# Attention scores as two full-height matmuls and two half-height ones, with the keys' halves placed to match and a new work plan

## The chip, the cores and the metric

The kernel runs on one core of a Trainium2 chip. The metric is the device time of one execution in microseconds. Before the change it was run three times, and one more execution was profiled.

## The reference, cut to what matters

One encoder layer works on two inputs, a prompt of 512 tokens and a sample of 1024 tokens, each token 1024 wide. RMSNorm is followed by one input projection whose columns are split into eight blocks. Group A is grouped-query attention (8 query heads, 2 key/value heads, 64 wide, normalised q and k, axial rotary). Group B is differential attention (4 heads with two softmax maps each, again 64 wide for q and k, 128 for v). Each group is gated by SiLU; the results are concatenated and projected back, the residual is added, and a last RMSNorm follows. The line that this change touches is the scores:

```
s = einsum('bqhgd,bkhd->bhgqk', q, k)          # group A, d = 64
s = einsum('bqhmd,bkhmd->bhmqk', q, k)         # group B, d = 64, two maps m
```

All values are float32.

## The kernel before, in words

Every float32 operand of a matmul is split into a high and a low half in float16, and products of halves are summed in float32. The projections use three products (high·high, high·low, low·high), one matmul each: `project_step`, lines 470 to 472.

For the scores, the contraction is only 64 long, so high and low are stacked: rows 0 to 63 of a q or k tile hold the high half of the 64 dimensions, and rows 64 to 127 hold the low half. `rows_high` (ACT) and `rows_low` (POOL) write these halves beside each other, a DMA transposes them, and q is stored to DRAM. `begin_tile` fetches q for one tile of 128 queries twice: `q1` as stored, and `q2` with the two halves of rows exchanged. One matmul of `q1` with the k tile sums high·high and low·low, one of `q2` sums low·high and high·low. A score op always fills two PSUM banks of 512 columns (`S[:, 0]` and `S[:, 1]`), so it is four matmuls of 128 rows, 128 columns of weights and 512 streamed columns, each with a weight load of its own: lines 1093, 1204 and 1205, 1241.

After a score op, DVE takes the row maximum (line 1098 or 1246), ACT takes the exponential (1109, 1255), in group B DVE combines two maps (1269), ACT and DVE or POOL split the result into halves (1064, 1067), a DMA transposes them into `pT` (1072), and PE multiplies `pT` with v: 24 small matmuls for one unit of work on the sample (lines 1122 to 1124 with 64 columns, 1283 to 1285 with 128).

The order of all work is computed when the kernel is built. Each piece is an `op` with an engine, an estimated duration, its inputs and its buffers; `Plan.schedule` plays the engines forward and writes the instructions out in that order. For PE the order comes from a list `seq`: attention units one after the other, the values of a unit `LAG` = 4 units behind its scores, and between them "fillers", the k steps (three matmuls each) of the projections ga, vb, kb, qb, gb and of the output projection. How many fillers come after each unit is set by `RATE_A` (group A, 80 units), `RATE_P` (group B, prompt, 16 units) and `RATE_S` (group B, sample, 32 units, two score ops each). The scores of group A make 80 score ops, those of group B 16 + 64, so 160 in all. There are 480 fillers for the projections and 200 for the output projection.

The stages on PE follow one another: the projections kva and qa; group A; group B on the prompt (called P below); group B on the sample (called S below); then the rest of the output projection.

Of the kernel before, what the change touches and what calls it, by code (L numbers as in the profile page):

```python
# [11 lines left out]
F16 = mybir.dt.float16  # L12
F32 = mybir.dt.float32
AF = mybir.ActivationFunctionType
ALU = mybir.AluOpType
AX = mybir.AxisListType

P = 128
D = 1024
KT = D // P  # L20
HD = 64
EPS = 1e-6
LAM_INIT = 0.8 - 0.6
NTP = 4
# [7 lines left out]
LAND = 1.0  # L32
SLACK = 1.03
NW = 15
RATE_A = 5.1
RATE_P = 4.0
RATE_S = 4.6
ET = mybir.EngineType
ALL = {ET.PE, ET.Activation, ET.DVE, ET.Pool, ET.SP}
MS = {ET.PE, ET.Activation, ET.DVE, ET.SP}  # L40
# [177 lines left out]
def kernel(ctx, tc, x_prompt, x_sample, g_norm, w_in, a_q_norm, a_k_norm,  # L218
                               lq1, lk1, lq2, lk2, b_subln, w_out, g_final, ropes, y_prompt, y_sample):
    nc = tc.nc  # L220
    ve, se, pe, ge, sy = nc.vector, nc.scalar, nc.tensor, nc.gpsimd, nc.sync
# [10 lines left out]
    qp = ctx.enter_context(tc.tile_pool(name="qp", bufs=2))  # L232
# [30 lines left out]
    k_a = [k_all[:, g] for g in range(3)]  # L263
# [222 lines left out]
    def pe_op(dur, fn, deps=(), uses=()):  # L486
        return op("PE", dur, fn, deps, uses)
# [285 lines left out]
    def rows_high(nh, box, kind="x4"):  # L773
        if kind == "x4":
            box["o2"] = rp.tile([P, 2, 8, P], F16, name="qk", tag="x4")
        elif kind == "xa":
            box["o2"] = tba.tile([P, 2, 8, P], F16, name="qka", bufs=2)
        else:
            box["o2"] = tba.tile([P, 1, 2, P], F16, name="kka", bufs=2)
        se.copy(box["o2"][:, 0, :nh, 0:HD], box["t1"][:, :nh, :])  # L780

    def rows_low(nh, box):
        o = box["o2"][:, 0]
        ge.tensor_tensor(out=o[:, :nh, HD:P], in0=box["t1"][:, :nh, :], in1=o[:, :nh, 0:HD], op=ALU.subtract)  # L784

    k_in, v_in, q_in = [None] * NT, [None] * NT, {}
    ka_b, va_b = buf("kav0"), buf("kav1")

    def post_kva(t, last, b):
        box = {}  # L790
        sq_b, t1_b, t2_b, x4_b = buf("sq"), buf("t1"), buf("t2"), buf("xk")
        tt, g, gi = t if t < NTP else t - NTP, t // 4, t % 4

        def vals():
            box["v"] = proj_ps["kva", t][:, P:2 * P].rearrange("p (h d) -> p h d", d=HD)
            box["k"] = proj_ps["kva", t][:, 0:P].rearrange("p (h d) -> p h d", d=HD)
            se.copy(v_a[t][:, :, 0:HD], box["v"])

        def vals_low():
            ve.tensor_tensor(out=v_a[t][:, :, HD:P], in0=box["v"], in1=v_a[t][:, :, 0:HD], op=ALU.subtract)  # L800

        def scale_rows():
            rope_add(2, box, ge)
            r = box["t1"]
            ge.tensor_tensor(out=r[:, :2, :], in0=r[:, :2, :],
                             in1=box["rs"].unsqueeze(2).broadcast_to([P, 2, HD]), op=ALU.mult)

        def turn():
            sy.dma_start_transpose(k_a[g][:, :, gi * P:(gi + 1) * P],
                                   box["o2"][:, 0, :2, :].rearrange("p h d -> p (h d)"))  # L810

        a = op("ACT", 0.25, vals, [last], [b])
        v_in[t] = op("DVE", 0.29, vals_low, [a], [b, va_b])
        s = op("ACT", 0.27, lambda: head_sums(box["k"], 2, box, "k"), [a], [b, sq_b])
        m = op("DVE", 0.55, lambda: head_var(2, box, "k", "eps_kva"), [s, w_ops["kva"][0]], [sq_b])
        r = op("POOL", 0.78, lambda: head_root(2, box, "k"), [m])
        ro = op("DVE", 0.6, lambda: rope_mult(box["k"], 2, rope_t["cak"][:, tt, :], rope_t["sak"][:, tt, :], 2, box),
                [a] + k_tables, [b, t1_b, t2_b])
        ad = op("POOL", 1.0, scale_rows, [ro, r], [t1_b, t2_b])
        h = op("ACT", 0.3, lambda: rows_high(2, box, "xk"), [ad], [t1_b, x4_b])  # L820
        lo = op("POOL", 0.43, lambda: rows_low(2, box), [h], [t1_b, x4_b])
        k_in[t] = op("SP", 0.4, turn, [lo], [x4_b, ka_b], kb=80, turn=True)
        tba_ops.extend((ro, k_in[t]))

    def post_rows(t, nm, last, b):

        box = {}
        nsub = 2 if nm == "qa" else 1
        kind = "xa" if nm == "qa" and t % 2 else "x4"
        t1_b, t2_b, x4_b = buf("t1"), buf("t2"), buf(kind)  # L830
# [202 lines left out]
    def begin_tile(t, half):  # L1033
        ts = TileState()
        ts.t, ts.half = t, half
        ts.T = 512 if t < NTP else 1024
        ts.kt0 = 0 if t < NTP else NTP
        ts.q_b, ts.o_b = buf("qp"), buf("O")
        ts.o = None

        def fetch():
            qd = q_dram[t][half]
            ts.q1 = qp.tile([P, 8, P], F16, name="q1")
            ts.q2 = qp.tile([P, 8, P], F16, name="q2")
            sy.dma_start(ts.q1, qd)
            sy.dma_start(ts.q2[0:HD], qd[HD:P])
            sy.dma_start(ts.q2[HD:P], qd[0:HD])
            ts.rs = tiny.tile([P, 8], F32, name="rs")

        ts.q_in = op("SP", 1.1, fetch, [q_in["qa" if half == 0 else "qb", t]], [ts.q_b], kb=512)  # L1050
        return ts

    def exps(st, i, p_i, S, w, ts, m, scale, nb):
        se.activation(p_i, S, AF.Exp, bias=nb, scale=scale, accum_out=ts.rs[:, m:m + 1])
# [26 lines left out]
    def plan_a(ts, hs):  # L1081
        t = ts.t
# [3 lines left out]

        def scores():
            st["S"] = ps_s.tile([P, 2, 512], F32, name="S", tag="S")
            for q, first in ((ts.q1, True), (ts.q2, False)):
                for j in range(2):  # L1090
                    h = hs[j % n]
                    g = 0 if t < NTP else 1 + j
                    pe.matmul(st["S"][:, j, :], q[:, h, :], k_a[g][:, h // 4, :], start=first, stop=not first)  # L1093

        def peak():
            S = st["S"]
# [27 lines left out]
                    pe.matmul(o, pT[:, 8 + c, :], v[:, kv, 0:HD], start=False, stop=(kt == nk - 1))  # L1124

        tiles = range(0, NTP) if t < NTP else range(NTP, NT)
        s = pe_op(0.87, scores, [ts.q_in] + [k_in[x] for x in tiles], [s_b, ts.q_b, ka_b])
        m = op("DVE", 1.4 if n == 1 else 1.55, peak, [s, qsc_in[t]], [s_b])
        e = op("ACT", 1.33 if n == 1 else 1.85, exp, [m], [s_b, p_b])
        tr, pT_b = plan_turn(st, e, p_b, "DVE")  # L1130
# [57 lines left out]
    def plan_b(ts, h):  # L1188
# [7 lines left out]
        if T == 512:  # L1196
# [2 lines left out]

            def scores():  # L1200
                st["S"] = ps_s.tile([P, 2, 512], F32, name="S", tag="S")
                for i in range(2):
                    kv = k_b[0, h][:, i, :]
                    pe.matmul(st["S"][:, i, :], ts.q1[:, 2 * h + i, :], kv, start=True, stop=False)
                    pe.matmul(st["S"][:, i, :], ts.q2[:, 2 * h + i, :], kv, start=False, stop=True)

            def peak():
                st["mx"] = tiny.tile([P, 2], F32, name="mx2")
# [10 lines left out]
                              accum_out=ts.rs[:, m:m + 1])  # L1219
                ps.append(p)  # L1220

            s = pe_op(0.87, scores, [ts.q_in] + ks, [s_b, ts.q_b] + kbufs)
            ss.append(s)
            m = op("DVE", 1.22, peak, [s, lam_in, w_ops["qb"][0]], [s_b])
            n = op("ACT", 0.38, bias, [m])
# [3 lines left out]
        else:  # L1229
            p_bs = []  # L1230
            for i in range(2):
# [4 lines left out]

                def scores(i=i, bx=bx):
                    bx["S"] = ps_s.tile([P, 2, 512], F32, name="S", tag="S")
                    for q, first in ((ts.q1, True), (ts.q2, False)):
                        for j, g in enumerate(groups):  # L1240
                            pe.matmul(bx["S"][:, j, :], q[:, 2 * h + i, :], k_b[g, h][:, i, :], start=first,  # L1241
                                      stop=not first)

                def peak(bx=bx):
                    bx["mx"] = tiny.tile([P, 1], F32, name="mx")
# [10 lines left out]
                                  accum_out=ts.rs[:, m:m + 1])  # L1256
                    ps.append(p)

                s = pe_op(0.87, scores, [ts.q_in] + ks, [s_b, ts.q_b] + kbufs)
                ss.append(s)  # L1260
                m = op("DVE", 1.22, peak, [s, lam_in, w_ops["qb"][0]], [s_b])
                n = op("ACT", 0.38, bias, [m])
# [232 lines left out]
    units = []  # L1495
    for t in range(NT):
        ts = begin_tile(t, 0)
        us = [plan_a(ts, hs) for hs in ([(h, h + 1) for h in range(0, 8, 2)] if t < NTP else [(h,) for h in range(8)])]
        plan_gate_a(ts, [u[2] for u in us], us[-1][1])
        units += [(u, RATE_A) for u in us]  # L1500
    for g in range(3):
# [71 lines left out]
```

## Time and profile before

| | before |
|---|---|
| median of 3 runs | 849.48 us (848.05 to 852.41) |
| profiled execution, its own time | 847.55 us |
| span from first to last instruction | 845.8 us |
| mean granted clock of TensorE | 0.987 |

The span is 1.75 us shorter than the profiled execution's time. In the profile, PE is TensorE's matmuls, PEld its weight loads, DVE, ACT and POOL the vector, scalar and GpSimd engines, SP the queue that issues every DMA. A matmul's row has a modelled end, so consecutive matmuls overlap in the rows, and their cost is read from start to start.

### The profile page before, as it was taken

Reading aid. Unit: us, or ns where it says so; the run is one execution under the profiler, and the core shown is the slowest. Engines: PE = TensorE matmul, PEld = TensorE weight load, DVE = VectorE, ACT = ScalarE, POOL = GpSimd, SP = SyncE. Lnnn points to the kernel's source line nnn. Section 1 sums busy time; section 2 is a strip of 40 time slices with the busy share of each in tenths; the row PEclk is TensorE's granted clock in tenths of the full one; section 3 lists DMA queues with packets and bytes.
Section 4 is the critical chain, followed back from the end, with each engine's and each line's share of the span. In section 5 each row is a group of like instructions: output and inputs, shape, how many; then the busy total and the mean of one; then the engine's idle time right before and its main releaser. Section 6 shows DMA issues by size and latency. Waiting matters only on the chain. (4 is left out here: it accounts for less than half of the span.)

```text
span 845.8 us, 16504 instructions
## 1 busy us (share of the span) xinstructions
PE 797.5 (94%) x6169; PEld 433.7 (51%) x6169; DVE 657.1 (78%) x1062; ACT 581.4 (69%) x1031; POOL 370.7 (44%) x377
## 2 busy tenths in 40 slices
PE   4999989999999999999999989899999999999885
PEld 2566634455555555555555445455555555555443
DVE  6888588687676878798777778677888999988832
ACT  6884259688568895567556866677888878777521
POOL 2689651000000104334253432345677777768830
PEclk9999989999999999999999999999999999999998
DMA  9999857999999999999999999989999988876942
GB/s 264 288 202 198 201 159 178 211 235 233 228 224 256 233 245 190 212 213 220 195 225 206 249 215 211 279 218 241 314 228 209 191 176 213 210 152 158 231 116 66
DMA packets 402448, 179.55 MB, mean 212 GB/s; under 512 B 364480, under 2 KB 365504, under 8 KB 402368
## 3 DMA queue, kind: packets, MB, share of 16 engines
q1 hardware_dynamic: 402368, 178.50, 94.5%
q8 instruction: 48, 0.79, 0.4%
q14 instruction: 32, 0.26, 0.1%
HBM read 62.33 MB, written 30.41 MB: 110 GB/s over the span
## 5 line engine op out<-in xcount | busy, mean ns | idle before, releaser
L1109 ACT ACTIVATE p<-S,nb,qsc 128x1024 f32<-128x1024 f32 (+1 forms) x96 | 101.4, 1058 | 74.1 <-DVE nb L1101 68.1
L1064 ACT CAST p<-p 128x1024 f16<-128x1024 f32 (+1 forms) x128 | 126.5, 989 | 35.5 <-DVE p L1269 22.2
L1098 DVE TENSOR_REDUCE mx<-S 128x1 f32<-128x1024 f32 (+1 forms) x80 | 97.5, 1219 | 31.9 <-PE S L1093 31.4
L1067 POOL TENSOR_TENSOR p<-p,p 128x1024 f16<-128x1024 f32 (+1 forms) x48 | 93.9, 1957 | 64.0 <-ACT p L1064 60.1
L1067 DVE TENSOR_TENSOR p<-p,p 128x1024 f16<-128x1024 f32 x80 | 102.4, 1282 | 23.5 <-ACT p L1064 23.1
L472 PEld LDWEIGHTS <-xT 128*128 128x128 f16 x672 | 66.2, 99 | 72.3 <-issue 3.1
L470 PEld LDWEIGHTS <-xT 128*128 128x128 f16 x672 | 66.7, 99 | 65.2 <-issue 5.6
L471 PEld LDWEIGHTS <-xT 128*128 128x128 f16 x672 | 66.2, 99 | 61.4 <-issue 3.7
L1246 DVE TENSOR_REDUCE mx<-S 128x1 f32<-128x1024 f32 x64 | 77.5, 1217 | 12.8 <-PE S L1241 12.3
L1093 PE MATMUL S<-ka,q 128*128 128x512 f16 x320 | 82.0, 379 | 2.2 <-ACT p L1109 2.1
L1421 PE MATMUL po<-wh_wo,mT 128*128 128x512 f16 (+1 forms) x200 | 75.4, 377 | 6.3 <-DMA mT<-ms 6.3
L771 POOL TENSOR_TENSOR t<-t,t 128x512 f32<-128x512 f32 (+1 forms) x36 | 48.1, 1336 | 72.5 <-DVE t L757 72.1
L1255 ACT ACTIVATE p<-S,nb,c_sc_b 128x1024 f32<-128x1024 f32 x64 | 76.8, 1200 | 2.5
L1422 PE MATMUL po<-wl_wo,mT 128*128 128x512 f16 (+1 forms) x200 | 75.4, 377 | 0.0
L1423 PE MATMUL po<-wh_wo,mT 128*128 128x512 f16 (+1 forms) x200 | 75.3, 376 | 0.0
L784 POOL TENSOR_TENSOR qk<-t,qk 128x512 f16<-128x512 f32 x30 | 37.2, 1243 | 80.4 <-ACT qk L780 79.3
L1241 PE MATMUL S<-kb,q 128*128 128x512 f16 x256 | 65.7, 379 | 5.2 <-ACT p L1255 4.5
L1122 PE MATMUL oa<-va,pT 128*128 128x64 f16 x640 | 64.2, 193 | 4.3 <-DMA pT<-p 4.1
L1149 POOL TENSOR_TENSOR sga<-sga,ca 128x512 f32<-128x512 f32 x12 | 14.4, 1206 | 121.5 <-DVE ca L1146 69.3
L1122 PEld LDWEIGHTS <-pT 128*128 128x128 f16 x640 | 57.5, 98 | 15.6 <-DMA pT<-p 7.2
L1124 PE MATMUL oa<-va,pT 128*128 128x64 f16 x640 | 64.2, 193 | 0.0
L1123 PE MATMUL oa<-va,pT 128*128 128x64 f16 x640 | 64.2, 193 | 0.0
(280 smaller groups left out, 2217.5 us busy)
## 6 DMA issues: line engine op xcount, KB each, us to landing
q<-qd SPq DMA_DIRECT2D x24, 256.0 KB, 3.4
q<-qd SPq DMA_DIRECT2D x48, 128.0 KB, 3.5
gd<-th SPq DMA_DIRECT2D x24, 256.0 KB, 3.4
out_dram<-xres SPq DMA_DIRECT2D x11, 512.0 KB, 3.2
qd<-qk SPq DMA_DIRECT2D x18, 256.0 KB, 3.3
xr<-in_x_sample_dram SPq DMA_DIRECT2D x8, 512.0 KB, 4.9
wst_wo<-in_w_out_dram SPq DMA_DIRECT2D x8, 512.0 KB, 5.5
xres<-in_x_sample_dram SPq DMA_DIRECT2D x8, 512.0 KB, 4.5
```

The costliest lines, as they stand in the source:

```text
L470: pe.matmul(ps[:, :n], xh[t][:, k, :], wh[:, k, :n], start=(k == 0), stop=False)
L1064: se.copy(st["o"][:, 0:T], st["p"][:, :T])
L1067: (ve if low_on == "DVE" else ge).tensor_tensor(out=st["o"][:, T:2 * T], in0=st["p"][:, :T], in1=st["o"][:, 0:T], op=ALU.subtract)
L1093: pe.matmul(st["S"][:, j, :], q[:, h, :], k_a[g][:, h // 4, :], start=first, stop=not first)
L1098: ve.tensor_reduce(st["mx"], S if n == 2 else S.rearrange("p a b -> p (a b)"), axis=AX.X, op=ALU.max)
L1109: se.activation(st["p"][:, w * j:w * j + w], Sf[:, w * j:w * j + w], AF.Exp, bias=st["nb"][:, j:j + 1], scale=qsc[t][:, h:h + 1], accum_ou ...
L1122: pe.matmul(o, pT[:, c, :], v[:, kv, 0:HD], start=(kt == 0), stop=False)
L1246: ve.tensor_reduce(bx["mx"], bx["S"].rearrange("p a b -> p (a b)"), axis=AX.X, op=ALU.max)
L1255: se.activation(p, bx["S"].rearrange("p a b -> p (a b)"), AF.Exp, bias=bx["nb"], scale=cst["sc_b"], accum_out=ts.rs[:, m:m + 1])
L1421: pe.matmul(ps[:, c], mh, blk.wh[:, k, c], start=(k == 0), stop=False)
L1422: pe.matmul(ps[:, c], mh, blk.wl[:, k, c], start=False, stop=False)
L1423: pe.matmul(ps[:, c], ml, blk.wh[:, k, c], start=False, stop=(k == KT - 1))
```

## The change

The score op becomes three partial products, not four. `q` is fetched so that `q[:, 0]` holds the high half in rows 0 to 63 and again in rows 64 to 127, and `q[:, 1]` the low half likewise; that takes two DMAs in place of three. A matmul of `q[:, 0]` with a k tile sums high·high and high·low. The low half of q then meets only the high half of k, in a matmul over 64 rows. For the two banks of a score op these two 64-row matmuls use different rows: bank 0 rows 0 to 63, bank 1 rows 64 to 127. So the k tile of bank 1 must have its high half in rows 64 to 127. `k_kind` says so by group of four token tiles: the prompt's tiles are "mixed" (even heads high first, odd heads low first), tiles 4 to 7 "high" (high first), tiles 8 to 11 "low" (low first); `sides` and `pairs` give `rows_high` and `rows_low` the matching views. In group A on the prompt, a unit now takes heads h and h + 4 (of the two different key heads) where it took h and h + 1. The planner's cost of a score op is 0.66 where it was 0.87, that of a q fetch 0.85 where it was 1.1, and two rates change.

```
-RATE_A = 5.1
+RATE_A = 4.8
-RATE_S = 4.6
+RATE_S = 5.2
...
-        se.copy(box["o2"][:, 0, :nh, 0:HD], box["t1"][:, :nh, :])
+        hi, _ = sides(box["o2"][:, 0, :nh, :], box["kind"])
+        se.copy(hi, pairs(box["t1"][:, :nh, :], box["kind"]))
     def rows_low(nh, box):
-        o = box["o2"][:, 0]
-        ge.tensor_tensor(out=o[:, :nh, HD:P], in0=box["t1"][:, :nh, :], in1=o[:, :nh, 0:HD], op=ALU.subtract)
+        hi, lo = sides(box["o2"][:, 0, :nh, :], box["kind"])
+        ge.tensor_tensor(out=lo, in0=pairs(box["t1"][:, :nh, :], box["kind"]), in1=hi, op=ALU.subtract)
+    def sides(o, kind):
+        if kind == "mixed":
+            o = o.rearrange("p (a b) (c d) -> p a (b c) d", b=2, c=2)
+            return o[:, :, 0:4:3, :], o[:, :, 1:3, :]
+        return (o[:, :, HD:P], o[:, :, 0:HD]) if kind == "low" else (o[:, :, 0:HD], o[:, :, HD:P])
+    def pairs(r, kind):
+        return r.rearrange("p (a b) d -> p a b d", b=2) if kind == "mixed" else r
+    def k_kind(t):
+        return ("mixed", "high", "low")[t // 4]
...
-            ts.q1 = qp.tile([P, 8, P], F16, name="q1")
-            ts.q2 = qp.tile([P, 8, P], F16, name="q2")
-            sy.dma_start(ts.q1, qd)
-            sy.dma_start(ts.q2[0:HD], qd[HD:P])
-            sy.dma_start(ts.q2[HD:P], qd[0:HD])
+            ts.q = qp.tile([P, 2, 8, P], F16, name="q")
+            for i in range(2):
+                sy.dma_start(ts.q[HD * i:HD * i + HD], qd.rearrange("(x d) h c -> d x h c", x=2))
...
+    def score(S, q, hs, ks):
+        for j in range(2):
+            pe.matmul(S[:, j, :], q[:, 0, hs[j], :], ks[j], start=True, stop=False)
+        for j in range(2):
+            r = slice(HD * j, HD * j + HD)
+            pe.matmul(S[:, j, :], q[r, 1, hs[j], :], ks[j][r], start=False, stop=True)
...
-        s = pe_op(0.87, scores, [ts.q_in] + ks, [s_b, ts.q_b] + kbufs)
+        s = pe_op(0.66, scores, [ts.q_in] + ks, [s_b, ts.q_b] + kbufs)
...
-        us = [plan_a(ts, hs) for hs in ([(h, h + 1) for h in range(0, 8, 2)] if t < NTP else [(h,) for h in range(8)])]
+        us = [plan_a(ts, hs) for hs in ([(h, h + 4) for h in range(4)] if t < NTP else [(h,) for h in range(8)])]
```

## Rows read from the trace of the kernel before

**Rows 1.** The page: busy time, then tenths in 40 slices.
```profile
PE 797.5 (94%) x6169; PEld 433.7 (51%) x6169; DVE 657.1 (78%) x1062; ACT 581.4 (69%) x1031; POOL 370.7 (44%) x377
...
PE   4999989999999999999999989899999999999885
...
PEclk9999989999999999999999999999999999999998
DMA  9999857999999999999999999989999988876942
```

**Rows 2.** Waits of PE: engine, line, releaser, us in total, times, longest.
```profile
PE warm L534 <- ACT xs L524: 9.0, 1, 9.0
PE po L1421 <- DMA mT<-ms: 6.3, 1, 6.3
PE S L1241 <- ACT p L1255: 4.5, 4, 2.7
PE oa L1122 <- DMA pT<-p: 4.1, 5, 1.8
```

**Rows 3.** The instructions that touch tile q, and its DMA issues.
```profile
L1093 PE MATMUL S<-ka,q x320: 376/379/380, 116.6 to 509.1; 128*128 128x512 f16 x160
L1241 PE MATMUL S<-kb,q x256: 376/379/379, 589.8 to 788.5; 128*128 128x512 f16 x128
...
L1204 PE MATMUL S<-kb,q x32: 376/379/379, 520.8 to 586.1; 128*128 128x512 f16 x32
...
L1045 SPq DMA_DIRECT2D q<-qd x24: 319/530/1040, 77.7 to 738.8; - x24
L1046 SPq DMA_DIRECT2D q<-qd x24: 455/456/541, 78.2 to 739.4; - x24
L1047 SPq DMA_DIRECT2D q<-qd x24: 587/588/1251, 78.7 to 739.9; - x24
```

**Rows 4.** Timeline of PE in group A: start us, us, engine, line.
```profile
301.75 1.03 PE L1093 MATMUL S<-ka,q 128*128 128x512 f16 x4
302.61 0.38 PE L470 MATMUL pj_vb<-wh_vb,xT 128*128 128x512 f16 x1
...
303.90 1.03 PE L1093 MATMUL S<-ka,q 128*128 128x512 f16 x4
304.77 0.19 PE L1122 MATMUL oa<-va,pT 128*128 128x64 f16 x1
304.80 0.19 PE L1123 MATMUL oa<-va,pT 128*128 128x64 f16 x1
...
305.47 0.38 PE L470 MATMUL pj_vb<-wh_vb,xT 128*128 128x512 f16 x1
```

**Rows 5.** Timeline of PE in stage S.
```profile
643.74 1.03 PE L1241 MATMUL S<-kb,q 128*128 128x512 f16 x4
644.60 0.22 PE L1283 MATMUL ob<-vb,pT 128*128 128x128 f16 x1
...
645.94 0.38 PE L1241 MATMUL S<-kb,q 128*128 128x512 f16 x1
```

**Rows 6.** Busy time by stretch: group A, stage S (clock, DMA share, GB/s last).
```profile
133.00:480.00 347.00, 342.49 (x3021) 181.41 (x3020) 269.45 (x419) 246.20 (x411) 75.92 (x56) 1.00 1.05 223
...
589.00:789.00 200.00, 193.25 (x1423) 108.81 (x1422) 178.20 (x219) 163.51 (x274) 145.45 (x138) 1.00 0.91 207
```

**Rows 7.** Busy time in 40 us inside group A and in stage S.
```profile
280.00:320.00 40.00, 39.90 (x368) 21.39 (x367) 32.46 (x47) 33.15 (x57) 3.77 (x3) 1.00 1.10 242
...
640.00:680.00 40.00, 39.98 (x293) 22.45 (x291) 35.81 (x44) 35.07 (x57) 31.82 (x32) 1.00 0.89 190
```

**Rows 8.** DVE's groups of instructions in stage S: count, busy us, mean ns.
```profile
L1433 DVE SCALAR_TENSOR_TENSOR xres<-po,mus,xres 128x512 f32<-128x512 f32 x17 | 12.6, 743 | 2.0 <-PE po L1423 1.9
L1491 DVE TENSOR_SCALAR xres<-xres,yrs 128x1024 f32<-128x1024 f32 x7 | 10.9, 1555 | 0.7 <-POOL yrs L251 0.7
```

**Rows 9.** Line 780 and line 784, the split into halves: ns min/median/max, first and last start.
```profile
L780 ACT CAST qk<-t x30: 603/616/619, 44.2 to 531.3; 128x512 f16<-128x512 f32 x30
L780 ACT CAST kka<-t x12: 282/297/298, 39.4 to 117.5; 128x128 f16<-128x128 f32 x12
...
L784 POOL TENSOR_TENSOR qk<-t,qk x30: 1148/1156/2138, 45.1 to 532.0; 128x512 f16<-128x512 f32 x30
L784 POOL TENSOR_TENSOR kka<-t,kka x12: 426/430/1268, 39.8 to 117.8; 128x128 f16<-128x128 f32 x12
```

**Rows 10.** Tile qk: its store to the keys' DRAM.
```profile
L865 SPq DMA_DIRECT2D kd<-qk x12: 525/593/1135, 329.7 to 432.3; - x12
```

**Rows 11.** Line 1072, the DMA transposes into pT.
```profile
L1072 SPq DMA_TRANSPOSE pT<-p x128: 1231/2733/6845, 131.8 to 802.7; - x128
...
DMA to landing us min/median/max: 3.5/4.9/8.9
```

**Rows 12.** What SP's DMA queue waited for.
```profile
SPq L1072 <- PE oa L1124: 45.5, 23, 3.5
SPq L1072 <- PE S L1093: 44.6, 21, 4.2
```

More of the change, by code (lines that the diff above doesn't have):

```diff
@@ L825, in post_rows @@
     def post_rows(t, nm, last, b):
-        box = {}
+        box = {"kind": k_kind(t) if nm == "kb" else "high"}
         nsub = 2 if nm == "qa" else 1
@@ L1042, in fetch @@
             qd = q_dram[t][half]
-            ts.q1 = qp.tile([P, 8, P], F16, name="q1")
-            ts.q2 = qp.tile([P, 8, P], F16, name="q2")
-            sy.dma_start(ts.q1, qd)
-            sy.dma_start(ts.q2[0:HD], qd[HD:P])
-            sy.dma_start(ts.q2[HD:P], qd[0:HD])
+            ts.q = qp.tile([P, 2, 8, P], F16, name="q")
+            for i in range(2):
+                sy.dma_start(ts.q[HD * i:HD * i + HD], qd.rearrange("(x d) h c -> d x h c", x=2))
             ts.rs = tiny.tile([P, 8], F32, name="rs")
-        ts.q_in = op("SP", 1.1, fetch, [q_in["qa" if half == 0 else "qb", t]], [ts.q_b], kb=512)
+        ts.q_in = op("SP", 0.85, fetch, [q_in["qa" if half == 0 else "qb", t]], [ts.q_b], kb=512)
         return ts
+    def score(S, q, hs, ks):
[4 more added lines that the diff above has]
+            pe.matmul(S[:, j, :], q[r, 1, hs[j], :], ks[j][r], start=False, stop=True)
     def exps(st, i, p_i, S, w, ts, m, scale, nb):
@@ L1088, in scores @@
             st["S"] = ps_s.tile([P, 2, 512], F32, name="S", tag="S")
[L1089 to L1093, printed above, removed]
+            hj = [hs[j % n] for j in range(2)]
+            score(st["S"], ts.q, hj, [k_a[0 if t < NTP else 1 + j][:, hj[j] // 4, :] for j in range(2)])
         def peak():
@@ L1126, in plan_a @@
         tiles = range(0, NTP) if t < NTP else range(NTP, NT)
-        s = pe_op(0.87, scores, [ts.q_in] + [k_in[x] for x in tiles], [s_b, ts.q_b, ka_b])
+        s = pe_op(0.66, scores, [ts.q_in] + [k_in[x] for x in tiles], [s_b, ts.q_b, ka_b])
         m = op("DVE", 1.4 if n == 1 else 1.55, peak, [s, qsc_in[t]], [s_b])
@@ L1201, in scores @@
                 st["S"] = ps_s.tile([P, 2, 512], F32, name="S", tag="S")
[L1202 to L1205, printed above, removed]
+                score(st["S"], ts.q, [2 * h, 2 * h + 1], [k_b[0, h][:, i, :] for i in range(2)])
             def peak():
@@ L1238, in scores @@
                     bx["S"] = ps_s.tile([P, 2, 512], F32, name="S", tag="S")
[L1239 to L1242, printed above, removed]
+                    score(bx["S"], ts.q, [2 * h + i] * 2, [k_b[g, h][:, i, :] for g in groups])
                 def peak(bx=bx):
@@ L1257, in exp @@
                     ps.append(p)
-                s = pe_op(0.87, scores, [ts.q_in] + ks, [s_b, ts.q_b] + kbufs)
+                s = pe_op(0.66, scores, [ts.q_in] + ks, [s_b, ts.q_b] + kbufs)
                 ss.append(s)
```

2 lines of the change are left out of this document (1 added, 1 removed).

## The prediction

> **What bounds the kernel now.** I read the page first, then the waits of PE, then the rows of tile q, then two stretches of PE's timeline, and last the busy time by stretch. The page has PE busy 94% of the span, DVE 78%, ACT 69%, POOL 44% [rows 1]; apart from the first slice and the last few, PE stands at 8 or 9 tenths everywhere, with the granted clock near full. A matmul's end is modelled, so busy time alone proves little. The waits are better evidence: the longest are 9.0 us before the first matmul and 6.3 us at the end for the last `mT`; everything between is a few us [rows 2]. So the kernel is a dense stream on PE, with a head and a tail that this change does not touch, and shortening it shortens the run, as long as the others keep up.
>
> What one piece costs comes from starts in the timeline. In group A a score op begins at 301.75 and the next matmul at 302.61: 0.86 us for four, 0.215 each. Between 302.61 and 303.90 lie six projection matmuls, again 0.215 each. The 24 matmuls of a unit's values take 304.77 to 305.47, 0.70 us, or 0.029 each with a weight load before every one [rows 4]. In S the values take 644.60 to 645.94, 1.34 us [rows 5]. A filler is three matmuls, 0.645.
>
> A unit of group A is then 0.86 + 0.70 + 5.1 x 0.645 = 4.85 us. The 80 score ops start between 116.6 and just under 509.1 [rows 3], 4.96 per unit: the stage is 98% what its matmuls need. A unit of S is 2 x 0.86 + 1.34 + 4.6 x 0.645 = 6.03 us. Its 64 score ops lie between 589.8 and 788.5 [rows 3], 31.5 units, 6.31 each: 96%. What is lost in S goes partly to PE waiting until ACT has read a score buffer, 4.5 us [rows 2].
>
> **The change, part by part.**
>
> *Scores.* Each of 160 ops has two full matmuls as before, and two over 64 rows, in different rows of the array and into different PSUM banks. If the two run side by side, they take the time of one: 0.215 saved per op, 160 x 0.215 = 34.4 us. The trace has no 64-row matmul, so the pair is bounded from both sides. Below: nothing on top of one matmul. Above: they run one after the other and nothing is saved. Within the case of overlap, the second starts later by between 0 and 0.029 us, the closest spacing of matmuls with new weights that the trace has [rows 4]. That row already streams 64 columns in its 0.029, so most of it is not issue; I take 0.010, which is 1.6 us in all (0 to 4.6).
>
> The Trainium skill (TensorE: Matmul & The Clock Gate, Part 3, packing by rows) says that matmuls in distinct row groups run concurrently, the next starting about 4 ns after the first. No row here shows it; an estimate from that page would make this term 0.6 us in place of 1.6.
>
> *Changing between full and half rows.* Each op goes from full-height matmuls to half-height ones and back: two changes. Below, a change costs nothing, as consecutive matmuls of different shapes do now: from 512 columns to 64 and back there is no gap in the starts [rows 4]. Above, the array empties first. A score matmul's row lasts 0.379 us [rows 3] where the next starts after 0.215, so emptying costs up to 0.164 per change. I take zero, the nearest row being the change of shape at 304.77 and 305.47, and keep the other end as a rival.
>
> The Trainium skill (TensorEngine Tiling (Array Packing), Key Properties) states that changing the tiling mode, not just the tile, drains TensorE, which speaks against this change. It gives no price, and no row of this trace has such a change. By its rule the time would be that of the emptying rival below.
>
> *New rates.* Group A gives up 80 x 0.3 = 24 fillers (15.5 us) to S and the end; S takes up 32 x 0.6 = 19. The sum on PE is unchanged. A new A unit is 0.655 + 0.70 + 4.8 x 0.645 = 4.45 us, a new S unit 2 x 0.655 + 1.34 + 5.2 x 0.645 = 6.00. What this alters is how tight the others are.
>
> In A, DVE is busy 269 of 347 us, 78%, and ACT 71% [rows 6]; a unit shorter by 0.4 us puts them near 84% and 77%. PE stays dense (39.9 of 40 us) where DVE has 81% and ACT 83% [rows 7], so I expect little loss: 0 to 7.6 us, the upper end if A falls from 98.7% busy to S's 96.6% over 360 us [rows 6]. I take 1.5.
>
> In S, DVE is busy 89% [rows 6], 5.62 us of each 6.31. A filler of the output projection brings about (2 x 0.743 + 1.555) / 16 = 0.19 us of DVE [rows 8], so 0.6 more make 5.73, and over 6.00 that is 95%. If DVE cannot go above its present 89%, a unit is 6.43 us, 0.43 over its matmuls where it now loses 0.28: 31.5 x 0.15 = 4.7 us lost. In one stretch of S, PE was fully busy with DVE at 90% [rows 7], so I take half, 2.5 (0 to 5). Shorter scores also give back some of the 4.5 us of waiting for score buffers; I count nothing for it.
>
> *The q fetch.* The same 512 KB in two DMAs, not three. SP's issues had medians of 0.53, 0.46 and 0.59 us [rows 3]; one less frees about 0.5 us of SP 24 times. SP already waits for PE with its transposes, 45 us for values to free `pT` and 45 us while scores run [rows 12], so I cost this at nothing. If two 64-row transfers landed a microsecond later than three, a fetch is still ordered well ahead of its first score; without that lead each of 24 tiles would lose that microsecond.
>
> *Transposes.* One lands 4.9 us after issue, 8.9 at worst [rows 11]. Values run four units behind scores; that is 17.8 us with the new unit, against about 1.2 + 0.2 + 1.4 + 1.0 + 1.3 us of maximum, bias, exponential and split plus the 4.9, so landing does not move to the path. SP needs 2.73 us per transpose to issue [rows 11], well inside 4.45.
>
> *Splits of k.* On the prompt the split is written in a crossed pattern: 4 ops on kva (0.30 us ACT, 0.43 POOL) and 4 on kb (0.62, 1.16) [rows 9]. Were each twice as long, ACT and POOL would carry 10 us more, none on the path: kb is stored by 432 and first used at 520.8 [rows 10, 3], and the prompt's kva long before 116. The other tiles only swap places. Heads h and h + 4 in a unit leave counts and sizes as they are.
>
> *Sum.* 847.55 (the profiled execution) - 34.4 + 1.6 + 1.5 + 2.5 = 818.75. Nothing else changes; the median of the runs shown is 1.9 above the profiled execution, 0.2%, inside their own spread. I predict **819 us**; with each small term at its end, 811 to 831.
>
> **The rivals.**
>
> *The pair runs in turn* (the change doesn't do what it says). The two half-height matmuls take 0.43 us, an op stays at 0.86, and only the order is new: 847.55 plus up to 2 for a plan built on a wrong cost, 849. For it: nothing in the trace shows two matmuls at once. Against it: they share neither rows nor bank. Chance 0.09.
>
> *The array empties at each change* (slower). Two changes of 0.164 cost 0.328 per op against 0.215 saved: 0.113 x 160 = 18 us, 866. It decides from 0.108 us per change upward. For it: the end of a matmul is that far behind the next start, and mixed heights have no row here. Against it: changes of column count are free [rows 4]. Chance 0.13. A cheap version, some 0.05 per change, keeps 0.115 per op, 18 us, and with the small terms ends near 834; chance 0.09.
>
> *Another engine becomes the bound.* If A cannot run with DVE above 81%, the highest it has in [rows 7], its 3.85 us of DVE per unit, less a little for fewer fillers, make 4.69 us where 4.56 is forecast, 79 x 0.13 = 10 us; with 4.7 in S it is 831. Against it: [rows 7] show PE not yet giving way at these shares. Chance 0.08.
>
> **How the numbers follow.** The main case has 0.61, and 819 is its time. A measurement of this kernel tells about 0.5% from no change (4.2 us). Faster: main, cheap changes and another engine, 0.61 + 0.09 + 0.08 = 0.78. Same: the pair in turn, 0.09. Slower: emptying, 0.13. The range goes from 811 to 848: it leaves out emptying, half of the pair in turn, and a little of the main case's lower tail.
>
> **What would show it.** Right: in the timeline, the third and fourth matmul of a score op start within 0.03 us of each other, the next matmul 0.215 after; a score op takes 0.65 to 0.67 us from start to start; the last score of group A starts near 479 and the first of S near 556; the scores of S stretch over 196 to 203 us, as before; PE's waits stay a few us each. Wrong: the fourth starts 0.215 after the third (in turn); a gap of 0.1 us or more before the third or before the matmul behind the fourth (emptying); the score op at 0.65 but idle PE, with DVE or ACT named as releaser (another engine); waits for q in front of the first score of a tile (the fetch).

## The result, and the profile after

| | before | after |
|---|---|---|
| median, four runs each on one chip | 848.93 us (848.05 to 852.41) | 858.84 us (856.97 to 862.1) |
| profiled execution, its own time | 847.55 us | 858.47 us |
| span | 845.8 us | 856.7 us |
| mean granted clock | 0.987 | 0.982 |

The ratio is 1.0113, with a 95% interval from 1.0071 to 1.0155. The forecast was 819 us; the kernel became slower by 1.1%.

The page of the kernel after, with the lines that answer to [rows 1]:

```profile
PE 798.8 (93%) x6169; PEld 406.4 (47%) x6169; DVE 667.0 (78%) x1062; ACT 579.1 (68%) x1031; POOL 362.2 (42%) x377
...
PE   4999979898999999998999896899989999999996
...
PEclk9999999999999999999999998999999999999999
DMA  9999958899999999999999996799999799998973
```

PE's busy time has not fallen (798.8 us, 797.5 in [rows 1]), and near slice 25 there is a hole in the PE and DMA lines that was not there before.

PE's timeline of the kernel after: a score op in group A, the stretch before group B, a score op in S (start us, us, engine, line).

```profile
303.83 0.38 PE L472 MATMUL pj_vb<-wh_vb,xT 128*128 128x512 f16 x1
304.04 0.59 PE L1069 MATMUL S<-ka,q 128*128 128x512 f16 x2
304.57 0.39 PE L1072 MATMUL S<-ka,q 64*128 64x512 f16 x2
304.89 0.39 PE L470 MATMUL pj_vb<-wh_vb,xT 128*128 128x512 f16 x1
...
522.11 0.19 PE L1142 MATMUL oa<-va,pT 128*128 128x64 f16 x1
528.58 0.61 PE L470 MATMUL pj_gb<-wh_gb,xT 128*128 128x512 f16 x1 [6.27 <-DVE t L757]
528.98 0.63 PE L471 MATMUL pj_gb<-wl_gb,xT 128*128 128x512 f16 x1
...
535.07 0.38 PE L472 MATMUL pj_gb<-wh_gb,xT 128*128 128x512 f16 x1
...
540.46 0.59 PE L1069 MATMUL S<-kb,q 128*128 128x512 f16 x2
...
640.84 0.59 PE L1069 MATMUL S<-kb,q 128*128 128x512 f16 x2
641.37 0.39 PE L1072 MATMUL S<-kb,q 64*128 64x512 f16 x2
641.69 0.39 PE L1433 MATMUL po<-wh_wo,mT 128*128 128x512 f16 x1
```

Three things stand in the two score ops. The two 64-row matmuls form one row of 0.39 us, and a single one lasts 0.386 (tile q, below), so they start within about 0.004 us of each other: that is what an overlap would look like, and an experiment below tests it. From the two full matmuls to this pair it is 0.53 us where two matmuls take 0.43 [rows 4]: 0.10 lost. From the pair to the next full matmul it is 0.32 where it should be 0.215: 0.105 lost. So a score op takes 0.85 us. Before, it took 0.86 to 0.87 [rows 4, 5]. These two ops stand for the rest: over all 160 score ops of this trace the median steps from start to start are 0.215, 0.311, 0.003 and, to the matmul behind the op, 0.318 us, so the two losses are 0.096 and 0.103, about 0.10 us each.

Tile q of the kernel after (ns min/median/max, first and last start):

```profile
L1069 PE MATMUL S<-ka,q x160: 376/379/389, 116.5 to 504.6; 128*128 128x512 f16 x160
L1072 PE MATMUL S<-ka,q x160: 386/387/387, 117.0 to 504.9; 64*128 64x512 f16 x160
L1069 PE MATMUL S<-kb,q x160: 376/379/634, 540.5 to 803.9; 128*128 128x512 f16 x160
L1072 PE MATMUL S<-kb,q x160: 386/386/605, 541.0 to 804.2; 64*128 64x512 f16 x160
```

With [rows 3], these starts divide the 10.9 us by which the span grew (the last score is the start of the last matmul of the last op, in both kernels):

| stretch | before, us | after, us | difference |
|---|---|---|---|
| start to last score of A | 509.1 | 504.9 | -4.2 |
| to first score of P | 11.7 | 35.6 | +23.9 |
| to last score of S | 267.7 | 263.7 | -4.0 |
| to the end of the span | 57.3 | 52.5 | -4.8 |

The loads of `kb`, P's and S's keys, before (line 1165) and after (line 1183):

```profile
L1165 SPq DMA_DIRECT2D kb<-kd x6: 324/522/877, 508.6 to 567.5; - x6
L1183 SPq DMA_DIRECT2D kb<-kd x6: 319/328/531, 535.5 to 595.2; - x6
```

The loss lies between group A and P. P's first score waits for its keys: their first load into `kb` was issued at 508.6 before and at 535.5 after. It needs one of the buffers that hold the inputs of the projections, and gb, the last projection, frees the first of them with its first eight steps. In the kernel after these are the 24 matmuls from 528.58 to the one that starts at 535.07; in the kernel before they had run before A's last score. At 5.1 fillers per unit, the plan gives group A 408 of them: the 384 of ga, vb, kb and qb, and 24 of gb. At 4.8 it gives 384, and no gb step is done when A ends. The list `seq` is the order that the planner wants; where an op cannot start yet, it puts a later one first, which is how other work comes to stand between A and P. In this stretch the timelines have 45 projection matmuls before and 96 after (51 x 0.215 = 11 us), 48 small value matmuls before and 120 after (2 us), and the new 6.3 us wait for DVE. The other 5 us are seven matmuls of gb at some 0.42 each (528.58 to 528.98 is the first such step), 1.5 us in all, and smaller waits.

Waits of PE in the kernel after (us in total, times, longest), to be held against [rows 2]:

```profile
PE oa L1140 <- DMA pT<-p: 11.8, 8, 4.1
PE warm L534 <- ACT xs L524: 9.0, 1, 9.0
PE pj_gb L470 <- DVE t L757: 6.3, 1, 6.3
PE pj_ga L470 <- DVE t L765: 4.9, 1, 4.9
```

Busy time by stretch in the kernel after (columns as in [rows 6]):

```profile
133.00:480.00 347.00, 335.48 (x2979) 165.16 (x2978) 274.44 (x417) 247.07 (x412) 63.95 (x51) 0.99 1.07 220
```

In group A, PE was busy 342.5 of 347 us [rows 6] and is now busy 335.5. A gave up 24 fillers (15.5 us) and 80 x 0.015 us of score time, 16.7 us together, but its last score is only 4.2 us earlier. Of the 12.5 us that are missing, 7.0 stand in these 347 us as idle PE.

### The profile page after: what moved, and what is told of

Read it like the earlier page. It is cut to its first block, busy times and chain, and to the rows that moved or that the text cites. A ratio compares the mean times of both kernels' runs of the same rounds, so it can differ in the third digit from the quotient of the medians.

```text
span 856.7 us, 16453 instructions
## 1 busy us (share of the span) xinstructions
PE 798.8 (93%) x6169; PEld 406.4 (47%) x6169; DVE 667.0 (78%) x1062; ACT 579.1 (68%) x1031; POOL 362.2 (42%) x377
## 4 chain that ended last, share of the span: by engine, by line
PE 62%; DVE 18%; DMA 10%; issue 4%; POOL 3%; ACT 2%; SPq 1%; POOLq 0%; DVEq 0%; ACTq 0%
DMA pT<-p 7%; PE S L1069 6%; PE S L1072 4%; PE po L1433 4%; PE po L1434 3%; PE po L1435 3%; PE pj_gb L470 3%; PE pj_vb L470 2%; PE pj_vb L471 2%; PE pj_vb L472 2%; PE pj_gb L471 2%; PE pj_gb L472 2%; PE oa L1140 2%; DVE mx L1116 2%; DVE mx L1258 2%
## 5 line engine op out<-in xcount | busy, mean ns | idle before, releaser
L1088 POOL TENSOR_TENSOR p<-p,p 128x1024 f16<-128x1024 f32 (+1 forms) x48 | 89.1, 1856 | 68.8 <-ACT p L1085 67.0
L1167 POOL TENSOR_TENSOR sga<-sga,ca 128x512 f32<-128x512 f32 x12 | 14.0, 1165 | 150.8 <-DVE ca L1164 92.9
L1140 PE MATMUL oa<-va,pT 128*128 128x64 f16 x640 | 65.1, 194 | 11.8 <-DMA pT<-p 11.8
L1433 PE MATMUL po<-wh_wo,mT 128*128 128x512 f16 (+1 forms) x200 | 74.5, 372 | 1.2 <-DVE th L914 1.2
L771 POOL TENSOR_TENSOR t<-t,t 128x512 f32<-128x512 f32 (+1 forms) x36 | 44.7, 1241 | 71.8 <-DVE t L757 66.0
L1435 PE MATMUL po<-wh_wo,mT 128*128 128x512 f16 (+1 forms) x200 | 74.1, 370 | 0.0
L1140 PEld LDWEIGHTS <-pT 128*128 128x128 f16 x640 | 56.3, 98 | 28.8 <-DMA pT<-p 14.9
L1281 DVE SCALAR_TENSOR_TENSOR p<-p,r,p 128x1024 f32<-128x1024 f32 (+1 forms) x48 | 61.8, 1287 | 2.1
L1141 PEld LDWEIGHTS <-pT 128*128 128x128 f16 x640 | 57.1, 98 | 1.4
```

The costliest lines, as they stand in the source:

```text
L1088: (ve if low_on == "DVE" else ge).tensor_tensor(out=st["o"][:, T:2 * T], in0=st["p"][:, :T], in1=st["o"][:, 0:T], op=ALU.subtract)
L1140: pe.matmul(o, pT[:, c, :], v[:, kv, 0:HD], start=(kt == 0), stop=False)
L1141: pe.matmul(o, pT[:, c, :], v[:, kv, HD:P], start=False, stop=False)
L1433: pe.matmul(ps[:, c], mh, blk.wh[:, k, c], start=(k == 0), stop=False)
L1435: pe.matmul(ps[:, c], ml, blk.wh[:, k, c], start=False, stop=(k == KT - 1))
```

## The experiments

Ratios are against the kernel before, run beside it on the same chip, with 95% intervals. Its own median went from 848.93 to 853.66 us over the chips and times, so kernels of different tables are best compared by their ratios. "Old rates" are 5.1 and 4.6, "new rates" 4.8 and 5.2. The planned duration is the one that the planner is given for a score op.

**The new scores alone.** The kernel after with the plan of before:

```
RATE_A, RATE_S = 5.1, 4.6;  pe_op(0.87, scores, ...);  op("SP", 1.1, fetch, ...)
```

> The changed kernel with the rates and the planned durations of the kernel before (5.1, 4.6; 0.87 for a score op, 1.1 for a q fetch). Theory (the scores gain almost nothing, the new plan loses the time): in the changed kernel's trace a score op takes 0.85 us from start to start against 0.865, 160 x 0.015 = 2.4 us, so this run is at 846.5 us, 845 to 848. Rival (another part of the change costs the time: the q fetch that lands in 4.1 us, not 3.5, or the crossed writes of k): the loss stays, 856 to 860.

849.59 us, ratio 0.9985 (0.996 to 1.001). The new scores, the fetch in two DMAs, the crossed split and the new heads change nothing that can be told; 160 x 0.015 = 2.4 us lies inside that interval.

**The new plan alone.** The kernel before with new rates, planned durations 0.66 and 0.85, and heads h, h + 4:

> The kernel before, its four full matmuls per score op and its q fetch, but planned as the changed kernel is (rates 4.8 and 5.2, 0.66 and 0.85, heads h and h + 4 in a unit on the prompt). Theory (the plan loses the time): 860 us, 857 to 864, with P's first score near 540 us and PE idle before it. Rival (the loss lies in the new instructions): 848 to 851.

861.03 us, ratio 1.0095 (1.0063 to 1.0127): the plan alone gives the whole loss. Tile q of this kernel:

```profile
L1093 PE MATMUL S<-ka,q x320: 376/379/634, 116.9 to 506.7; 128*128 128x512 f16 x160
...
L1204 PE MATMUL S<-kb,q x32: 379/379/634, 542.3 to 598.1; 128*128 128x512 f16 x32
```

Its score ops are four full matmuls, and yet it has the same 35.6 us between A's last and P's first score, where the kernel before has 11.7.

**Rates or planned duration?** The new scores with each of the two set back:

```
new_scores_old_rates:   RATE_A, RATE_S = 5.1, 4.6;  planned 0.66
true_cost_new_rates:    RATE_A, RATE_S = 4.8, 5.2;  planned 0.85
true_cost_old_rates:    RATE_A, RATE_S = 5.1, 4.6;  planned 0.85
true_cost_only_rate_S:  RATE_A, RATE_S = 5.1, 5.2;  planned 0.85
new_scores_087:         RATE_A, RATE_S = 5.1, 4.6;  planned 0.87
```

> The changed kernel with only the two rates put back to 5.1 and 4.6; the planner still believes in 0.66 for a score op. Theory one (the rates lose the time, because group A no longer carries the first gb projections that P's keys wait for): 846 to 850. Theory two (the planned duration that is 0.19 too short loses it, by an order that doesn't fit): 855 to 860.

> The changed kernel with its new rates, but with the planned duration of a score op set to the 0.85 us that the traces show, not 0.66. Theory (the wrong duration spoils the order, as the run with old rates and 0.66 at 865.8 against old rates and 0.87 at 849.6 has it): most of the loss goes, 847 to 853. Rival (the new rates cost by themselves too, since group A ends before the first gb projections): 855 to 860, with P's first score still near 540 us.

> The changed kernel with old rates and 0.85 for a score op, and the new 0.85 for a q fetch: it differs from the run with the whole old plan by 0.02 us per score op and 0.25 us per q fetch in the planner alone. Theory (what counts is that the planned durations are near the true ones): 847 to 852, as with the old plan. Rival (any other set of durations gives another order, and the order of before was a lucky one): above 855.

> true_cost_new_rates (852.8) with RATE_A back at 5.1, RATE_S still 5.2. Theory (RATE_A at 4.8 lets group A end before the first gb projections have freed the buffers for P's keys, and that is what the new rates lose): P's first score near 515 us and 842, 839 to 846. Rival (RATE_S loses it): 849 to 856.

> true_cost_old_rates with 0.87 in place of 0.85 for a score op, nothing else. Theory (the order is sensitive to hundredths of a us in the plan, some us either way): anywhere from 840 to 852. Rival (near true durations give the same time): within 2 us of 841.9.

| rates of A and S | planned 0.66 | planned 0.85 | planned 0.87 |
|---|---|---|---|
| 5.1, 4.6 | 865.82, 1.0169 (1.0136 to 1.0203) | 841.87, 0.9921 (0.9895 to 0.9947) | 846.89, 0.9955 (0.9937 to 0.9974) |
| 5.1, 5.2 | - | 846.47, 0.9972 (0.9943 to 1.0001) | - |
| 4.8, 5.2 | 858.84, 1.0113 (1.0071 to 1.0155) | 852.78, 1.0031 (0.9997 to 1.0064) | - |

The theory that the rates alone cost the time fell: with the old rates and the planned 0.66, the time is the worst of the table. A planned duration that is not the true one costs under both pairs of rates. With the true one, the rates do cost, 1.1% by the ratios; about half comes with RATE_A (1.0031 to 0.9972) and half with RATE_S (0.9972 to 0.9921), and the intervals of neighbours just touch. With 0.85 planned, P's first score is at 537.5 with RATE_A 4.8, and at 515.9 and 513.3 with 5.1. How far such times depend on the exact order is seen in the first row and in the first experiment: from planned 0.85 and 0.85 to 0.87 and 1.1, for a score op and a fetch, the ratio goes from 0.9921 to 0.9985. So the parts don't add up neatly, and no exact price of a rate follows from them.

**Is the gain of that table the new scores'?** The kernel before, old rates, planned 0.85, fetch 0.85, heads h, h + 4:

> The kernel before with its four full matmuls, planned as the run true_cost_old_rates was (0.85 for a score op that takes 0.865, 0.85 for a q fetch, heads h and h + 4, old rates). That run was at 841.9 where the new scores can account for 2.4 us of the 8. Theory (the rest is the order that this set of durations happens to give): 842 to 846. Rival (the new scores are worth more than their op shows): 848 to 852.

841.63 us, ratio 0.9895 (0.9874 to 0.9916). The four full matmuls are as fast in this order as the new scores (0.9921). Both beat the kernel before and the kernel after, and what they gain is the order's.

**Do the halves run side by side?** The kernel after, both half-height matmuls in the same rows:

```
-            r = slice(HD * j, HD * j + HD)
+            r = slice(0, HD)
```

> The changed kernel with both half-height matmuls of a score op on rows 0 to 63; bank 1's third product then meets rows 0 to 63 of its key tile, which is the low half for half of the keys, so part of the scores is left out there. If the two half-height matmuls of the changed kernel truly run side by side because their rows differ, the fourth now starts 0.215 us after the third and a score op takes 0.85 + 0.215 = 1.065 us; 160 of them add 34 us, 885 to 895. If they ran side by side whatever their rows, or if the row starts deceive, the op stays at 0.85 and the time within 5 us of the changed kernel's.

PE's timeline of this kernel:

```profile
599.99 0.59 PE L1069 MATMUL S<-kb,q 128*128 128x512 f16 x2
600.51 0.60 PE L1072 MATMUL S<-kb,q 64*128 64x512 f16 x2
601.05 0.39 PE L470 MATMUL pj_gb<-wh_gb,xT 128*128 128x512 f16 x1
```

The pair's row is now 0.60 long, the second starting 0.21 after the first, and the op takes 1.06 us. So in the kernel after they do overlap. One execution took 877.28 us, 18.4 over the kernel after, for 160 x 0.21 = 34 us more of PE's work; 885 to 895 was expected, so even added work does not come out in full.

**Is the loss one of the change of height, or of each half-height matmul?** First, the score ops of two units of A as one op, four full matmuls and then four half-height ones, planned 1.5, old plan otherwise; in a second kernel the two score ops of a unit of S likewise. Then, the old plan with the order full, half, full, half:

```
two_ops_one_change_A:  for each of the two ops: 2 full;  then for each of the two ops: 2 half
four_changes:
         for j in range(2):
             pe.matmul(S[:, j, :], q[:, 0, hs[j], :], ks[j], start=True, stop=False)
-        for j in range(2):
             r = slice(HD * j, HD * j + HD)
             pe.matmul(S[:, j, :], q[r, 1, hs[j], :], ks[j][r], start=False, stop=True)
```

> The new scores in the old plan, but in group A the score ops of two units are one piece of work: four full-height matmuls, then the four half-height ones. If the 0.095 us into half height and 0.11 back are paid per change and not per matmul, such a double op takes 4 x 0.215 + 2 x 0.215 + 0.2 = 1.49 us against 2 x 0.85 = 1.70, and 40 of them save 8 us over the same plan without it (849.6): 841.5, 839 to 845, unless holding both score buffers at once makes PE wait. Rival (the gap belongs to each half-height pair): 1.70 per double op and 848 to 852.

> The same in group A and also for the two maps of a head in stage S (32 more double ops). If the cost is per change and buffers allow it: another 32 x 0.21 = 6.7 us, 835, 833 to 840. Rival: with both score buffers filled by one op, PE cannot start the next pair until ACT has read both; one pair then holds them for about 1.5 + 1.2 + 0.4 + 1.2 + 1.2 + 0.2 = 5.7 us plus queueing on DVE and ACT out of 6.1 us per unit, so S gets longer than its 199 us, 850 or more.

> The new scores in the old plan, with the four matmuls of a score op in the order full, half, full, half: four changes of height instead of two, and the half-height ones no longer beside each other. Theory (each change costs 0.095 to 0.11 us): full to half 0.31, half to full 0.32, so 1.26 us per op from start to start. Rival (the gap has to do with the bank being written again, or with two matmuls at once, and not with the height): 0.86 to 1.07.

PE's timeline of the kernel with double ops in A:

```profile
293.30 1.03 PE L1068 MATMUL S<-ka,q 128*128 128x512 f16 x4
294.26 0.61 PE L1072 MATMUL S<-ka,q 64*128 64x512 f16 x4
294.80 0.20 PE L1142 MATMUL oa<-va,pT 128*128 128x64 f16 x1
```

PE's timeline of the kernel with four changes:

```profile
304.29 0.38 PE L1070 MATMUL S<-ka,q 128*128 128x512 f16 x1
304.60 0.39 PE L1071 MATMUL S<-ka,q 64*128 64x512 f16 x1
304.92 0.39 PE L1070 MATMUL S<-ka,q 128*128 128x512 f16 x1
305.24 0.39 PE L1071 MATMUL S<-ka,q 64*128 64x512 f16 x1
305.56 0.20 PE L1139 MATMUL oa<-va,pT 128*128 128x64 f16 x1
```

The loss belongs to the change of height. A double op takes 1.50 us, two of the kernel after 1.70: one pair of changes less, 0.20 saved. With four changes, each step from one height to the other takes 0.31 or 0.32 in place of 0.215, and an op takes 1.27. As kernels, none is of use: four changes 893.22 us (one execution), double ops in A 861.39, ratio 1.0148 (1.012 to 1.0176), double ops in A and S 892.89, ratio 1.0532 (1.0487 to 1.0578). A double op fills both score buffers at once, and in the last of these kernels PE waits 13.0 us for ACT to read a score buffer, where the kernel after has 2.4. Why the double ops in A alone miss the expected 841.5 us by 20 is not shown.

**What would a score op without the loss have brought?** One full-height matmul on bank 0 in place of the two half-height ones, so that no height changes; then only the two matmuls of the high half of q:

```
-        for j in range(2):
-            r = slice(HD * j, HD * j + HD)
-            pe.matmul(S[:, j, :], q[r, 1, hs[j], :], ks[j][r], start=False, stop=True)
+        pe.matmul(S[:, 0, :], q[:, 1, hs[0], :], ks[0], start=False, stop=True)
three_full:            plan of the kernel after
three_full_old_rates:  RATE_A, RATE_S = 5.1, 4.6;  planned 0.66
two_full_old_rates:    RATE_A, RATE_S = 5.1, 4.6;  planned 0.44;  the added line left out
```

> The changed kernel, its plan untouched, with a full-height matmul on bank 0 in place of the two half-height ones; bank 0 gets low times low on top, and bank 1's product of low q with high k is left out. A score op is then three matmuls and no change of height: 0.645 us, what the plan assumes. Theory (the plan fits a kernel whose change of height is free, and the 0.2 us per op undoes it): the sum of the prediction holds, 819, 812 to 830. Rival (the new rates leave group B's start without work for PE whatever a score op costs): 832 to 845, with PE idle around 500 to 540 us.

> three_full (score op of three full-height matmuls, 0.645 us; bank 1's product of low q with high k left out) with the old rates 5.1 and 4.6, and its planned 0.66 now true. It takes 160 x 0.22 = 35 us of PE work out of old_scores_near_plan (841.6). Theory one (PE sets the pace, and three_full was held up by its rates): 805 to 818. Theory two (the stream on PE is not what sets the pace alone: DVE, ACT and the transposes cannot be compressed as far, so shorter scores come back in part): 822 to 840.

> The same plan and rates with only the two full-height matmuls of q's high half per score op, 0.43 us, planned at 0.44 (every product of low q with high k is left out). Another 34 us of PE work go. Theory one (PE sets the pace): a further 30 to 34 us below three_full_old_rates. Theory two (the others set it): within 10 us of three_full_old_rates, with DVE's busy share near 80% or more and PE's waits for pT, DVE and ACT grown.

| | us per score op | median, us | ratio (interval) | PE busy, us |
|---|---|---|---|---|
| three_full | 0.645 | 847.89 | 0.997 (0.995 to 0.999) | 771.8 |
| three_full_old_rates | 0.645 | 854.02 | 1.0044 (1.0017 to 1.0072) | 774.2 |
| two_full_old_rates | 0.43 | 854.01 | 1.005 (1.0026 to 1.0075) | 749.7 |

Against the kernel before, 35 or 70 us less of matmuls bring nothing; the two kernels with three matmuls came out above every range that was expected for them. But these kernels also have other orders than the kernel before, so the cleaner comparison is with the new scores in the same order, planned at 0.66. There an op that is 0.205 us cheaper (33 us in all) brings 1.0113 down to 0.997 with the new rates, some 12 us, and 1.0169 (new_scores_old_rates) down to 1.0044 with the old ones, some 11 us. About a third of the work taken out comes out as time. The order planned at 0.66 is itself a slow one, 865.82 against 841.87 us for the same kernel planned at 0.85; what the cheap op would bring in that better order was not tried. Waits of PE and the busy time of group A in the kernel with two matmuls:

```profile
PE oa L1137 <- DMA pT<-p: 17.7, 10, 5.2
PE S L1069 <- ACT p L1264: 14.6, 13, 3.0
PE ob L1292 <- DMA pT<-p: 14.2, 9, 6.1
PE S L1069 <- ACT p L1124: 12.1, 13, 1.9
```

```profile
120.00:500.00 380.00, 338.89 (x2978) 179.13 (x2977) 291.36 (x453) 265.26 (x447) 76.07 (x60) 0.95 1.03 215
```

PE now waits for transposes and for ACT to free score buffers, 59 us in these four rows, against 4.1 + 1.8 and 4.5 + 2.1 us for the same causes before. The granted clock is 0.95 in A, so part of A's matmuls ran at the lower level, 1.2 GHz, as well. An estimate from that row: 0.05 x 380 / 0.5 = 38 us of A at that level, where a matmul takes twice as long (0.42 us against 0.215, last section), so up to 19 us of what was taken out went there.

**What holds group A, then?** Three kernels built on three_full_old_rates: the transposes of half size (the high half used again for the low one), DVE's maximum in A over half of the scores (with q's scale and a constant of the exponent changed to suit), and both.

```
half_transpose:
-            sy.dma_start_transpose(st["pT"][:, 0:2 * T // P, :], st["o"][:, 0:2 * T])
+            sy.dma_start_transpose(st["pT"][:, 0:T // P, :], st["o"][:, 0:T])
half_maximum:
-  ve.tensor_reduce(st["mx"], S if n == 2 else S.rearrange("p a b -> p (a b)"), axis=AX.X, op=ALU.max)
+  ve.tensor_reduce(st["mx"], S if n == 2 else S[:, 0, :], axis=AX.X, op=ALU.max)
```

> three_full_old_rates (854.0) with the transposes into pT of half the size: only the high half of the probabilities is transposed, and the product of its low half with v is replaced by the high half again, so PE's work, DVE's, ACT's and the plan are the same and only DMA traffic (256 KB less of 512 in each of 96 large transposes, 128 of 256 in the small ones) and SP's issue time fall. Theory (the transposes, through SP's issue and the DMA engines, set the pace of group A once scores are short): group A well below its 396 us, 820 to 838. Rival (not DMA): 849 to 856.

> three_full_old_rates with DVE's maximum over 512 of the 1024 scores in group A on the sample (64 times some 0.6 us less, 38 us of DVE; the maximum leaves half of the scores out, and the scores are scaled by a tenth and their bias lowered so that all stays finite). Theory (DVE's chain from scores to exponential sets the pace of group A): group A shorter by 15 us or more, 825 to 842. Rival (DVE is not it): 849 to 856.

> Both at once. If one of them sets the pace, the time is that of the better single one or lower. If each hid the other: clearly below both, 800 to 825. If neither moves it, what is left is the order itself: engines wait in the order that the planner wrote, not for a busy engine; 848 to 856.

| | median, us | ratio (interval) | last score of A, us |
|---|---|---|---|
| three_full_old_rates | 854.02 | 1.0044 (1.0017 to 1.0072) | 513.0 |
| half_transpose | 840.2 | 0.9859 (0.9822 to 0.9895) | 503.4 |
| half_maximum | 855.47 | 1.0034 (1.0008 to 1.006) | 514.4 |
| half_both | 833.74 | 0.9782 (0.9748 to 0.9815) | 496.8 |

The transposes and the busy time of group A, first in three_full_old_rates:

```profile
L1091 SPq DMA_TRANSPOSE pT<-p x128: 1231/2894/7367, 130.5 to 805.9; - x128
```

```profile
120.00:500.00 380.00, 355.82 (x3085) 186.20 (x3084) 293.17 (x456) 264.16 (x445) 81.57 (x62) 0.98 1.04 215
```

and then with half the size:

```profile
L1091 SPq DMA_TRANSPOSE pT<-p x128: 1188/1267/4035, 130.6 to 790.0; - x128
```

```profile
120.00:500.00 380.00, 363.90 (x3171) 191.79 (x3172) 299.24 (x464) 266.30 (x450) 87.01 (x64) 0.99 0.77 171
```

Halving the transposes takes the DMA engines' share in group A from 1.04 to 0.77 and SP's issue from 2.89 to 1.27 us; PE's waits for `pT` no longer stand among its longest, and 14 us are gained by the medians (1.0044 to 0.9859), 9.6 of them before A's last score. Without that, less work for PE had left the DMA share in A where it was: 1.05 [rows 6], 1.04 with three matmuls, 1.03 with two. Less work for DVE brings nothing by itself and 6 us on top of the half transposes. The shares of the DMA engines and of SP's issue are not told apart by this.

## Why the prediction was wrong

**Changing between full and half rows: the step that failed.** The prediction took zero from the nearest row, the change of column count, and kept emptying as a rival at 0.164 per change with break-even at 0.108. The rival was right that a change costs, and its size was too large: 0.096 and 0.103 us, just under break-even. The op saves 0.015 us where 0.205 was forecast, and the term of 34.4 - 1.6 us shrank to 2.4. The row that priced it at zero had no change of height in it. That the time rose, as this rival had it, is no merit of the rival: at the measured price the change would still have saved 2.4 us, and the rise is the plan's.

The Trainium skill (TensorEngine Tiling (Array Packing), Key Properties) says that a change of the tiling mode drains TensorE. The runs agree that such a change has a cost, paid per change and not per matmul, 0.10 us into and 0.10 us out of 64 rows. That the array empties in that time they do not show: the 64-row matmul at 304.60 of the kernel with four changes starts 0.07 us before the modelled end of the row in front of it.

**The overlap** was right: 0.010 us was taken for the second matmul's delay, and it is 0.003 to 0.004.

**New rates: the second step that failed.** "The sum on PE is unchanged" is true of the work and not of the order. Losses of 1.5 and 2.5 us were forecast, and the rival "in turn" allowed "up to 2 for a plan built on a wrong cost"; the plan alone costs the old scores 0.95%, 8 us. What was missed is that A's fillers beyond 384 are the first steps of gb, on which P's keys wait, and that another planned duration is another order: planned at 0.66, the new scores take 865.82 us with the old rates, planned at 0.85 they take 841.87. A duration that fits does not make the order good either, for the op of three_full and three_full_old_rates does take 0.645. Why the order planned at 0.66 is slow stays open.

**"Shortening it shortens the run": the step beneath both.** The prediction read a stream that is 94% busy, with few waits, as the bound. The runs with less of PE's work say otherwise: in the same order, 33 us less bring 11 or 12. Had the change of height been free, this plan would still not have given 819 us, as three_full shows with 847.89. The evidence against "another engine becomes the bound" was a single stretch of 40 us in which PE stayed dense [rows 7]; that rival had 0.08 and stopped at 831. It asked about DVE, and DVE's maximum, halved alone, gave nothing. What the same rows showed and the prediction passed over is the DMA engines' share of 1.05 over group A [rows 6], and the line of nines [rows 1]; it also called SP's 2.73 us of issue per transpose "well inside 4.45". That transposes hold part of group A is shown by the 14 us. That leaves 840 us where PE's matmuls would allow less; whether the rest is the order's or another engine's stays open.

**Priced at nothing, rightly:** the fetch and the splits of k. With the old plan the whole of the new scores comes to 0.9985, and PE waits for no q. "Values run four units behind scores" was to cover the transposes' landing; PE's waits of 11.8 us for `pT` in the kernel after, 4.1 before [rows 2], say that it does not everywhere.

## What to carry to other kernels

Price an operation with no row in the trace by a small kernel of its own, or put the main chance on the bound that has a mechanism: two half-height matmuls side by side save 0.215 us, and going there and back costs 0.20, so they pay only where many of them follow one another and the buffers allow it. A busy share of 94% is not a bound until work taken out of that engine, in the same order, shortens the run by as much. Where a planner sets the order, a planned duration can cost more than the change is worth (24 us here between 0.66 and 0.85 for the same kernel), so run the old code under the new plan and the new code under the old one before a gain or loss is put down to either.

## What the runs showed of the hardware

Weight loads do not run ahead over a change of height. PE's weight loads in the kernel after, at the score op of S shown above:

```profile
640.63 0.31 PEld L1069 LDWEIGHTS <-q 128*128 128x128 f16 x2
641.36 0.10 PEld L1072 LDWEIGHTS <-q 64*128 64x128 f16 x2 [0.42 <-issue]
641.68 0.10 PEld L1433 LDWEIGHTS <-mT 128*128 128x128 f16 x1 [0.23 <-issue]
641.70 0.10 PEld L1434 LDWEIGHTS <-mT 128*128 128x128 f16 x1
```

The load of line 1069 starts at 640.63 for the matmul at 640.84, and that of 1434 at 641.70 for one at 641.91: 0.21 us ahead. The load into 64 rows (641.36) and the one after it (641.68) start 0.01 us before their matmuls at 641.37 and 641.69. So load and matmul start together, and the 0.10 us lost at a change passes before either; what PE waits for in it, no row names. Inside half height, loads do run ahead. This is the double op in A, whose half-height matmuls start at 294.26:

```profile
294.26 0.12 PEld L1072 LDWEIGHTS <-q 64*128 64x128 f16 x4 [0.42 <-issue]
```

All four loads lie in its first 0.12 us, those of the second pair too, whose matmuls start some 0.22 us later.

After the idle stretch from 522.1 to 528.6 the first matmuls of gb come 0.42 us apart, twice the 0.215 of the rest, which is the lower level of 1.2 GHz; the granted clock was 0.74 between 520 and 530. A wait of 6.3 us costs more than itself.
